# Unread products ahead of each tile of the MLPs' first products, and second products in three matmuls per block

## The chip, the cores and the metric

The kernel runs on one core of one Trainium2 chip. The metric is the device time of one execution in microseconds (us). The core has a tensor engine (PE in the profile, its weight loads as PEld), a vector engine (DVE), a scalar engine (ACT), a general engine (POOL) and an engine that issues transfers (SP).

## The reference

One launch computes three transformer layers on 256 tokens of width 1024: `first_block` (one layer) and `second_block` (two layers and a last norm). Each layer is a mixer with a residual and an MLP with a residual, and the MLP is what the change touches:

```python
D_FF = 4 * D_MODEL
...
        h = _rmsnorm(x, ln_mlp_g[l])
        x = x + jnp.square(jax.nn.relu(h @ w_mlp_up[l])) @ w_mlp_down[l]
...
def squared_relu_mlp(h, w_up, w_down):
    return jnp.square(jax.nn.relu(h @ w_up)) @ w_down
...
        x = x + squared_relu_mlp(rmsnorm(x, norm_mlp[layer]), w_up[layer], w_down[layer])
```

So there are three MLPs. In each the first product takes 1024 features to 4096, the second takes 4096 back to 1024. Everything is fp32.

## The kernel before, in words

**Layout.** Activations lie feature by feature: `x` is eight blocks of 128 features (partitions) by 256 tokens (columns). All weights stand in one stream `w` of 128x128 blocks in the order in which they are used. `load` (L134, on SP) brings two units of eight blocks into a tile `stg`; `take` splits a unit into two parts whose sum is the fp32 value: ACT writes the high part `whi` (L185), DVE the rest `wlo` (L187), both of type fp32r, which TensorE takes at one pass. Activations are split in the same way (`xh` and `xl`, one tile named `xo`; `hid` in the MLPs).

**One product of blocks.** `gemm` makes one output tile of 128 features by 256 tokens in a bank of PSUM (`pg`). For each block of weights it issues three matmuls of 256 columns: high weights by high activations (L242), high by low (L245), low by high (L246). Each matmul instruction loads its 128x128 weights anew (its LDWEIGHTS is in the profile as PEld). `gemm1` makes one such tile, `gemm2` two in one tile of PSUM, `gemm_tokens` (L281) makes tiles with the two operands in each other's place: activations are loaded, weights are streamed.

**The MLP** (`mlp`, three times: `mlp("norm_mix0")`, `mlp("norm_mix1")`, `mlp(None)`; MLP 1, 2 and 3 below). The first products are 16 calls of `gemm2`, so 32 output tiles of 8 blocks each, 256 blocks. ACT and DVE then make `hid` from each pair. The second products are 8 output tiles of 32 blocks each, again 256 blocks, followed by the residual. So each half of an MLP is 256 blocks, and with three matmuls per block it is 768 matmuls.

**The wide form.** In the second products `WIDE_NOT` says for how many of the eight tiles `gemm` is used. For MLP 1 and MLP 3 it is all eight; for MLP 2 it is one, and the other seven tiles go through `gemm_wide`: two matmuls per block, one of 512 columns (high weights by both parts of `hid`, L254) and one of 256 columns (L255). Its result stands in two halves, which an ACT copy (L400) and a DVE addition (L401) bring together.

**What sets the order.** The tile framework schedules the instructions of each engine from the program; PE runs them in that order. Other matmuls of the kernel, which the prediction uses for comparison, are fp32 products, which the profile shows as two records each: the sums of squares (L339 and L340, 128x256, weights of ones), `rstd_tokens` (L352, one column), and `decays` (L756, 128 columns). L961 is a lone fp32r product of 256 columns in the second mixer.

Of the kernel before, what the change touches and what calls it, by code (L numbers as in the profile page):

```python
# [10 lines left out]
FP32 = mybir.dt.float32  # L11
# [3 lines left out]
AF = mybir.ActivationFunctionType  # L15
ALU = mybir.AluOpType
PSUM = bass.MemoryType.PSUM

T = 256
D = 1024  # L20
FF = 4096
KD = 8
# [11 lines left out]
UNIT = 8  # L34
CHUNK_UNITS = 2

WIDE_NOT = {"norm_mix0": 8, "norm_mix1": 1, None: 8}

FIRST = 256

# [3 lines left out]
LEAD = 16  # L44
ROOM = 128
MIXED = 56

GROUPS_MIX = [range(0, 8)]
GROUPS_ATT = [range(0, 4), range(4, 6), range(6, 8)]
# [31 lines left out]
def kernel(  # L81
# [11 lines left out]
    nc = tc.nc  # L93
    nosync = mybir.DependencyInfo(mybir.DependencyClass.NoSync, mybir.DependencyReason.DATA)

    def after(first, last):
        if last is not None:
            tc.add_manual_dep(first.ins, last.ins.name, nosync)

    def pool(name, bufs=1, space=None, stack=ctx):  # L100
        kw = {"space": space} if space is not None else {}
        return stack.enter_context(tc.tile_pool(name=name, bufs=bufs, **kw))
# [7 lines left out]
    pg_p = pool("pg", 4, PSUM)  # L110
# [10 lines left out]
    def placed(t, n, at):  # L121

        return t[:, at:at + n * T].rearrange("p (k t) -> p k t", k=n)

    xh, xl = placed(xo, KD, LEAD), placed(xo, KD, LEAD + KD * T)
    cst = keep.tile([128, NCONST], FP32, name="cst")
    ones = keep.tile([128, 128], FP32, name="ones")
# [10 lines left out]
    a = 0  # L138
    for k, cols in ((2, slice(0, FIRST)), (5, slice(FIRST, UW)), (8, slice(UW, CW))):
# [3 lines left out]
        a = e  # L143
# [24 lines left out]
    units = {}  # L168
# [6 lines left out]
    def take(u, pieces=2):  # L175

        c, i = divmod(u, CHUNK_UNITS)
        if c not in staged:
            load(c)
        src = staged[c][:, i * UW:(i + 1) * UW]  # L180
        h = whi_p.tile([128, UW], FP32R, name="whi")
        l = wlo_p.tile([128, UW], FP32R, name="wlo")
        n = UW // pieces
        pieces = [slice(q * n, (q + 1) * n) for q in range(pieces)]
        act = [nc.scalar.activation(out=h[:, z], in_=src[:, z], func=AF.Copy)  # L185
               for z in (pieces if u == 0 else [slice(0, UW)])]
        dve = [nc.vector.tensor_tensor(out=l[:, z], in0=src[:, z], in1=h[:, z], op=ALU.subtract) for z in pieces]  # L187
        chain = hold.pop(0) if hold else None
        if chain:
            after(act[0], chain[0])  # L190
            after(dve[0], chain[1])
        units.clear()
        units[u] = h, l

    def block(n=1):

        b = stream["block"]
        stream["block"] = b + n
        u, i = divmod(b, UNIT)
        assert i + n <= UNIT  # L200
        if u not in units:
            take(u)
        h, l = units[u]
        return h[:, i * 128:(i + n) * 128], l[:, i * 128:(i + n) * 128]
# [13 lines left out]
    def step():  # L218
        for c in list(chains):
            if next(c, "end") == "end":  # L220
                chains.remove(c)

    def slot(steps=1):
        for d in list(due):
            d[0] -= 1
            if d[0] <= 0:
                due.remove(d)
                d[1]()
        credit[0] = credit[0] + steps if chains else 0
        while credit[0] >= 1:  # L230
            credit[0] -= 1
            step()

    def drain():
        while due or chains:
            slot()

    def gemm(ps, ks, ah, al, prev=None):

        for k in ks:  # L240
            h, l = block()
            m0 = nc.tensor.matmul(out=ps, lhsT=h, rhs=ah[:, k], start=(k == ks[0]), stop=False)  # L242
            if k == ks[0]:
                after(m0, prev)
            nc.tensor.matmul(out=ps, lhsT=h, rhs=al[:, k], start=False, stop=False)  # L245
            m1 = nc.tensor.matmul(out=ps, lhsT=l, rhs=ah[:, k], start=False, stop=(k == ks[-1]))  # L246
        return m1

    def gemm_wide(kt, a):

        ps = pg_p.tile([128, 2, T], FP32, name="pg")
        for k in range(kt):
            h, l = block()
            nc.tensor.matmul(out=ps, lhsT=h, rhs=a[:, k], start=(k == 0), stop=False)  # L254
            nc.tensor.matmul(out=ps[:, 1], lhsT=l, rhs=a[:, k, 0], start=False, stop=(k == kt - 1))  # L255
        slot(kt / KD)
        return ps

    def gemm1(kt, ah, al, steps=1):
        ks = kt if isinstance(kt, range) else range(kt)  # L260
        ps = pg_p.tile([128, 2, T], FP32, name="pg")
        gemm(ps[:, 0], ks, ah, al)
        slot(steps * len(ks) / KD)
        return ps[:, 0]

    def gemm2(kt, ah, al):
        ps = pg_p.tile([128, 2, T], FP32, name="pg")
        m = gemm(ps[:, 0], range(kt), ah, al)
        gemm(ps[:, 1], range(kt), ah, al, prev=m)
        slot(2 * kt / KD)  # L270
        return ps
# [72 lines left out]
    rvar = keep.tile([128, T], FP32, name="rvar")  # L344
# [25 lines left out]
    def mlp(gain_next):  # L370
        def variance():
            u = tmp.tile([128, 512], FP32, name="rs_u", bufs=1)[:, 0:T]
            nc.vector.tensor_scalar(out=u, in0=sum_squares(), scalar1=1.0 / D, scalar2=EPS, op0=ALU.mult, op1=ALU.add)
            nc.vector.reciprocal(out=rvar, in_=u)

        variance()
        with ExitStack() as st:
            hp = pool("hid", stack=st)
            mp = pool("mlpt", 2, stack=st)
            hid = hp.tile([128, FF // 128, 2, T], FP32R, name="hid")  # L380
            for j in range(0, FF // 128, 2):
                ps = gemm2(KD, xh, xl)
                r = mp.tile([128, 2, T], FP32, name="r")
                s = mp.tile([128, 2, T], FP32, name="s")
                nc.scalar.activation(out=r, in_=ps, func=AF.Relu)
                nc.scalar.activation(out=hid[:, j:j + 2, 0], in_=r, func=AF.Square)
                nc.vector.scalar_tensor_tensor(out=s, in0=ps, scalar=0.0, in1=r, op0=ALU.max, op1=ALU.mult)
                nc.vector.tensor_tensor(out=hid[:, j:j + 2, 1], in0=s, in1=hid[:, j:j + 2, 0], op=ALU.subtract)
            for j in range(KD):

                wide = j < KD - WIDE_NOT[gain_next]
                if wide:
                    ps = gemm_wide(FF // 128, hid)
                else:
                    ps = gemm1(FF // 128, hid[:, :, 0], hid[:, :, 1])

                for z in HALVES if gain_next is None and j == KD - 1 else [slice(0, T)]:
                    t = tmp.tile([128, T], FP32, name="dn")[:, z]
                    if wide:
                        nc.scalar.activation(out=t, in_=ps[:, 1], func=AF.Copy)  # L400
                        nc.vector.tensor_tensor(out=t, in0=ps[:, 0], in1=t, op=ALU.add)  # L401
                    nc.vector.tensor_tensor(out=t, in0=t if wide else ps[:, z], in1=rvar[:, z], op=ALU.mult)  # L402
                    nc.vector.tensor_tensor(out=x[:, j, z], in0=t, in1=x[:, j, z], op=ALU.add)  # L403
                    if z.stop - z.start < T:
                        nc.scalar.activation(out=rstd[:, z], in_=x[:, j, z], func=AF.Square)  # L405
                if gain_next is not None:
                    operand(j, gain_next)
                    squares(j)
                else:
                    if j < KD - 1:  # L410
                        squares(j)
                    nc.scalar.activation(out=xg[:, j], in_=x[:, j], func=AF.Copy, scale=v_("norm_final", j))  # L412
# [132 lines left out]
    with ExitStack() as st:  # L545
# [14 lines left out]
        ps = gemm1(KD, xh, xl)  # L560
# [159 lines left out]
        for j in range(0, 4, 2):  # L720
            ps = gemm2(KD, xh, xl)
            z = hg.tile([128, 2, T], FP32, name="hz", bufs=1)
# [83 lines left out]
        for j in range(4):  # L806
# [4 lines left out]
            t = hg.tile([128, T], FP32, name="ut", bufs=2)  # L811
# [8 lines left out]
            t = hg.tile([128, T], FP32, name="ut", bufs=2)  # L820
# [9 lines left out]
        for b, (yh, yl) in enumerate(((yc_h, yc_l), (ya_h, ya_l), (yh_h, yh_l))):  # L830
            if b == 2:
                while "linear" not in events:
                    slot()
                mhp = pool("mixh", stack=late)
                mh = placed(mhp.tile([128, KD * T + ROOM], FP32R, name="mh"), KD, MIXED)
                ml = placed(mhp.tile([128, KD * T + ROOM], FP32R, name="ml"), KD, MIXED)
            gates = {}
# [9 lines left out]
            for j in range(0, KD, 2):  # L847
                if j + 2 < KD:
                    gate(j + 2)
                ps = gemm2(4, yh, yl)  # L850
# [22 lines left out]
    for turn in (4096.0, 1.0):  # L873
# [4 lines left out]
        for i in range(6):  # L878
            m, e = math.frexp(rest)
# [14 lines left out]
    with ExitStack() as st:  # L894
# [10 lines left out]
        ps = gemm1(KD, xh, xl)  # L905
# [82 lines left out]
    with ExitStack() as st:  # L988
# [95 lines left out]
        ps = gemm1(KD, xh, xl)  # L1084
        scaled(kr[0:32], ps[0:32])
        a, b = rope(kr, 32)
# [4 lines left out]
        for j in range(2):  # L1091
            ps = gemm1(3, cqh, cql, RA)
            zr = att.tile([128, T], FP32, name="zr", bufs=2)
            nc.scalar.activation(out=zr, in_=ps, func=AF.Copy, scale=mscale)
            a, b = rope(zr, 128)
            for i in range(4):
                nc.vector.tensor_tensor(out=qm[64:96, 4 * j + i], in0=a[32 * i:32 * i + 32], in1=b[32 * i:32 * i + 32],
                                        op=ALU.add)
        for j in range(4):
            ps = gemm1(3, cqh, cql, RA)  # L1100
# [5 lines left out]
        for j in range(4):  # L1106
            ps = gemm1(2, ckh, ckl, rate[0])
# [22 lines left out]
    for z, (pool_, name) in zip(HALVES, ((po_p, "po"), (sc_p, "sc"))):  # L1130
        ps = pool_.tile([128, 512], FP32, name=name)[:, 0:T // 2]
# [204 lines left out]
```

## Time and profile before

| what | us |
|---|---|
| median of 3 runs | 1070.21 |
| lowest and highest of the runs | 1070.03 and 1076.8 |
| the profiled execution | 1071.9 |
| span of the profiled execution (first to last instruction) | 1070.1 |
| PE busy in the span | 1046.7 (98%) |
| DVE, ACT, POOL busy | 830.4, 597.9, 161.3 |
| mean granted TensorE clock, share of full speed | 0.995 |

The profile is of one execution. Busy times of PE add up matmuls that overlap, so the rate of PE is read from the distance between the starts of its instructions and not from its busy share. MLP 1 stands at about 289 to 467 us of the span, MLP 2 at 597 to 767, MLP 3 at 894 to 1060; the second half of each begins at about 376, 676 and 980 us.

### The profile page before, as it was taken

The numbers are of one execution on the slowest core, as the hardware profiler recorded it, in microseconds if no ns is written. First come the engines' busy times: TensorE is split into PE (matmuls) and PEld (weight loads), VectorE is DVE, ScalarE is ACT, GpSimd is POOL, SyncE is SP. The second block draws the span as 40 slices with busy tenths as digits, with TensorE's granted clock in tenths as the row PEclk, the third lists the DMA queues.
The fourth block names the chain that finished last, engine by engine and source line by source line (L and its number), as shares of the span: only waits on it lengthen the run. The fifth ranks groups of instructions, "written<-read, shape, count | busy, mean of one in ns | idle before, by whom it ended". The sixth has DMA issues, their size and how long they took to land. (4 is left out here: it accounts for less than half of the span.)

```text
span 1070.1 us, 21172 instructions
## 1 busy us (share of the span) xinstructions
PE 1046.7 (98%) x8584; PEld 1025.5 (96%) x8584; DVE 830.4 (78%) x1599; ACT 597.9 (56%) x930; POOL 161.3 (15%) x174
## 2 busy tenths in 40 slices
PE   7999999999999999999999999999999999999996
PEld 6999998999999999999999999988999999999996
DVE  7999898987897666669878977666699789776563
ACT  6467456666475544446655565444458755555441
POOL 1044651110500001120001200011121013000120
PEclk9999999999999999999999999999999999999998
DMA  8644433455445555555343555555454334555541
GB/s 291 225 159 153 148 130 119 163 197 181 174 173 200 181 195 177 190 189 193 119 157 122 196 197 190 175 190 194 158 182 156 136 112 156 205 193 183 197 179 40
DMA packets 29010, 183.99 MB, mean 172 GB/s; under 512 B 3056, under 2 KB 6384, under 8 KB 7280
## 3 DMA queue, kind: packets, MB, share of 16 engines
q1 hardware_dynamic: 28768, 182.50, 48.1%
q8 instruction: 67, 1.10, 0.4%
q14 instruction: 31, 0.25, 0.1%
q10 hardware_dynamic: 144, 0.13, 0.0%
HBM read 181.57 MB, written 1.05 MB: 171 GB/s over the span
## 5 line engine op out<-in xcount | busy, mean ns | idle before, releaser
L187 DVE TENSOR_TENSOR wlo<-stg,whi 128x512 fp32r<-128x512 f32 (+1 forms) x676 | 469.7, 736 | 156.9 <-ACT whi L185 152.3
L185 ACT ACTIVATE whi<-stg 128x1024 fp32r<-128x1024 f32 (+1 forms) x340 | 356.1, 1051 | 327.4 <-PE pg L245 266.1
L242 PE MATMUL pg<-xo,whi 128*128 128x256 f32 x1472 | 415.0, 283 | 8.3 <-ACT whi L185 7.3
L245 PE MATMUL pg<-xo,whi 128*128 128x256 f32 x1472 | 413.9, 282 | 0.6 <-DVE xo L319 0.6
L246 PE MATMUL pg<-xo,wlo 128*128 128x256 f32 x1472 | 413.9, 282 | 0.4 <-DVE wlo L187 0.2
L242 PEld LDWEIGHTS pg<-xo,whi 128*128 128x128 f32 x1472 | 278.9, 190 | 9.6 <-ACT whi L185 7.6
L245 PEld LDWEIGHTS pg<-xo,whi 128*128 128x128 f32 x1472 | 279.6, 190 | 2.2 <-DVE xo L319 1.3
L246 PEld LDWEIGHTS pg<-xo,wlo 128*128 128x128 f32 x1472 | 278.5, 189 | 1.9 <-DVE wlo L187 1.5
L246 PE MATMUL pg<-hid,wlo 128*128 128x256 f32 x544 | 151.6, 279 | 0.0
L245 PE MATMUL pg<-hid,whi 128*128 128x256 f32 x544 | 151.6, 279 | 0.0
L242 PE MATMUL pg<-hid,whi 128*128 128x256 f32 x544 | 151.6, 279 | 0.0
L245 PEld LDWEIGHTS pg<-hid,whi 128*128 128x128 f32 x544 | 103.2, 190 | 0.0
L242 PEld LDWEIGHTS pg<-hid,whi 128*128 128x128 f32 x544 | 102.3, 188 | 0.0
L246 PEld LDWEIGHTS pg<-hid,wlo 128*128 128x128 f32 x544 | 102.1, 188 | 0.0
L254 PE MATMUL pg<-hid,whi 128*128 128x512 f32 x224 | 79.2, 397 | 0.0
L327 POOL TENSOR_TENSOR sqa<-xv 128x256 f32<-128x256 f32 x6 | 5.0, 831 | 455.5 <-DVE xv L403 291.2
L255 PE MATMUL pg<-hid,wlo 128*128 128x256 f32 x224 | 62.9, 281 | 0.0
L331 POOL TENSOR_TENSOR sq<-xv 128x256 f32<-128x256 f32 x36 | 29.9, 836 | 173.5 <-DVE xv L403 160.5
L254 PEld LDWEIGHTS pg<-hid,whi 128*128 128x128 f32 x224 | 42.1, 188 | 10.4
L281 PE MATMUL pg<-whi,xo 128*128 128x256 f32 x256 | 47.4, 282 | 0.0
L255 PEld LDWEIGHTS pg<-hid,wlo 128*128 128x128 f32 x224 | 42.0, 188 | 0.0
L281 PEld LDWEIGHTS pg<-whi,xo 128*128 128x128 f32 x256 | 39.5, 188 | 0.1
(356 smaller groups left out, 1599.1 us busy)
## 6 DMA issues: line engine op xcount, KB each, us to landing
stg<-w SPq DMA_DIRECT2D x168, 1024.0 KB, 4.8
t<-t_bias SPq DMA_DIRECT2D x8, 128.0 KB, 3.0
cb<-chk_bias SPq DMA_DIRECT2D x1, 1024.0 KB, 4.8
xv<-x_in SPq DMA_DIRECT2D x2, 384.0 KB, 6.7
cst<-consts SPq DMA_DIRECT2D x1, 640.0 KB, 11.2
stg<-w SPq DMA_DIRECT2D x1, 512.0 KB, 8.1
out<-xg SPq DMA_DIRECT2D x2, 256.0 KB, 2.5
stg<-w SPq DMA_DIRECT2D x1, 384.0 KB, 6.8
```

The lines of the kernel that those rows point to most:

```text
L185: act = [nc.scalar.activation(out=h[:, z], in_=src[:, z], func=AF.Copy) for z in (pieces if u == 0 else [slice(0, UW)])]
L187: dve = [nc.vector.tensor_tensor(out=l[:, z], in0=src[:, z], in1=h[:, z], op=ALU.subtract) for z in pieces]
L242: m0 = nc.tensor.matmul(out=ps, lhsT=h, rhs=ah[:, k], start=(k == ks[0]), stop=False)
L245: nc.tensor.matmul(out=ps, lhsT=h, rhs=al[:, k], start=False, stop=False)
L246: m1 = nc.tensor.matmul(out=ps, lhsT=l, rhs=ah[:, k], start=False, stop=(k == ks[-1]))
L254: nc.tensor.matmul(out=ps, lhsT=h, rhs=a[:, k], start=(k == 0), stop=False)
L255: nc.tensor.matmul(out=ps[:, 1], lhsT=l, rhs=a[:, k, 0], start=False, stop=(k == kt - 1))
L281: nc.tensor.matmul(out=ps, lhsT=a[:, k, t], rhs=w_, start=(k == 0 and i == 0), stop=(k == kt - 1 and i == 2))
L327: nc.gpsimd.tensor_tensor(out=sqa, in0=x[:, j], in1=x[:, j], op=ALU.mult)
L331: nc.gpsimd.tensor_tensor(out=s, in0=x[:, j], in1=x[:, j], op=ALU.mult)
```

## The change

Two edits. First, `gemm` may issue an unread product ahead of the first matmul of a tile: `mlp` fills a list `between` with 32 entries, one for each tile of its first products, and empties it before the second products. The product writes the first columns of the tile's own bank, and the tile's first matmul then overwrites them. An entry is a kind, a number of columns n and, in some, how many times. The kind "dense" loads high weights and streams n columns of `xh`, "tokens" loads 128 columns of `xh` and streams n columns of the high weights (both fp32r), "exact" loads ones and streams n columns of constants (both fp32). Second, the wide form is gone: all second products are made of three matmuls per block.

```diff
-WIDE_NOT = {"norm_mix0": 8, "norm_mix1": 1, None: 8}
+B = ("tokens", 240)
+_ds = [("dense", 16), ("exact", 1), ("dense", 128), ("exact", 128), ("tokens", 128), ("dense", 100), ("tokens", 256), ("exact", 64)]
+BETWEEN = {
+    "norm_mix0": [k for d in _ds for k in (d, B, d, B)],
+    "norm_mix1": [k for d in _ds for k in (d, d, B, d)],
+    None: [k for d in (("tokens", 240, 2), ("tokens", 200), ("tokens", 136), ("tokens", 248), ("tokens", 256, 2),
+                       ("tokens", 256, 4), ("tokens", 224), ("tokens", 240, 3)) for k in (d, d, B, d)],
+}
...
+    between = []
+
+    def small(ps, prev):
+
+        kind, n, times = (between.pop(0) + (1,))[:3]
+        h = next(iter(units.values()))[0]
+        for _ in range(times):
+            a, b = {"tokens": (xh[:, 0, 0:128], h[:, 0:n]), "dense": (h[:, 0:128], xh[:, 0, 0:n]),
+                    "exact": (ones, cst[:, 0:n])}[kind]
+            m = nc.tensor.matmul(out=ps[:, 0:n], lhsT=a, rhs=b, start=True, stop=True)
+            after(m, prev)
+            prev = m
+        return prev
+
     def gemm(ps, ks, ah, al, prev=None):
 
         for k in ks:
             h, l = block()
+            if k == ks[0] and between:
+                prev = small(ps, prev) if between[0] else between.pop(0) or prev
             m0 = nc.tensor.matmul(out=ps, lhsT=h, rhs=ah[:, k], start=(k == ks[0]), stop=False)
...
+            between[:] = BETWEEN[gain_next]
             for j in range(0, FF // 128, 2):
                 ps = gemm2(KD, xh, xl)
...
+            between.clear()
             for j in range(KD):
-
-                wide = j < KD - WIDE_NOT[gain_next]
-                if wide:
-                    ps = gemm_wide(FF // 128, hid)
-                else:
-                    ps = gemm1(FF // 128, hid[:, :, 0], hid[:, :, 1])
+                ps = gemm1(FF // 128, hid[:, :, 0], hid[:, :, 1])
```

`gemm_wide` itself, the ACT copy and the DVE addition that belonged to it are removed.

The lines of `gemm` move: L242, L245 and L246 of before are L266, L269 and L270 of after, and an unread product has L255. PE of after, at a border of two tiles in the first products of MLP 1, where the product is an "exact" one of one column (`cst` and `ones` are its operands, the number behind `pg` tells the two tiles of PSUM apart):

```order
L270 MATMUL pg_3741<-xo_87,wlo_3775 128x256
L255 MATMUL pg_3810<-cst_88,ones_89 128x1
L266 MATMUL pg_3810<-xo_87,whi_3811 128x256
L269 MATMUL pg_3810<-xo_87,whi_3811 128x256
L270 MATMUL pg_3810<-xo_87,wlo_3812 128x256
```

One product stands between the last matmul of one tile and the first of the next, and it writes the next tile's bank; before, the two tiles followed each other there without it. Each of the 96 tiles of the three first halves gets such an entry. 84 entries are one product, the other 12 (all in MLP 3) two, three or four in a row, which makes 32 products in MLP 1, 32 in MLP 2 and 53 in MLP 3. 15 of them are "exact" (6 in MLP 1, 9 in MLP 2), 102 are fp32r.

PE of before, at the border from the first to the second products of MLP 2 (`hid` is the hidden activations, the 128x512 rows are the wide form):

```order
L245 MATMUL pg<-xo,whi 128x256
L246 MATMUL pg<-xo,wlo 128x256
L254 MATMUL pg<-hid,whi 128x512
L255 MATMUL pg<-hid,wlo 128x256
L254 MATMUL pg<-hid,whi 128x512
```

PE of after, inside the same second products:

```order
L270 MATMUL pg<-hid,wlo 128x256
L266 MATMUL pg<-hid,whi 128x256
L269 MATMUL pg<-hid,whi 128x256
L270 MATMUL pg<-hid,wlo 128x256
L266 MATMUL pg<-hid,whi 128x256
```

The 224 blocks that had two matmuls have three, and the number of columns per block is the same 768.

## Rows read from the trace of the kernel before

**Rows 1.** Windows, MLP stretches: busy us (instructions) by engine, clock, DMA share, GB/s.

```profile
300.00:374.00 74.00, 74.00 (x630) 74.00 (x630) 56.00 (x95) 45.56 (x57) 0.00 (x0) 1.00 0.55 198
677.00:754.00 77.00, 77.00 (x438) 66.86 (x437) 50.71 (x81) 34.23 (x42) 9.01 (x11) 1.00 0.53 189
985.00:1058.00 73.00, 73.00 (x647) 73.00 (x646) 40.06 (x61) 28.11 (x31) 12.39 (x13) 1.00 0.42 147
```

**Rows 2.** First matmul of each block in seven MLP stretches: count, ns, first and last start.

```profile
L242 PE MATMUL pg<-xo,whi x210: 281/281/281, 299.8 to 373.7; 128*128 128x256 f32 x105
...
L242 PE MATMUL pg<-hid,whi x241: 281/281/281, 380.0 to 464.8; 128*128 128x256 f32 x121
...
L242 PE MATMUL pg<-xo,whi x213: 276/276/276, 601.7 to 673.9; 128*128 128x256 f32 x107
...
L254 PE MATMUL pg<-hid,whi x219: 397/397/398, 676.6 to 753.7; 128*128 128x512 f32 x110
...
L242 PE MATMUL pg<-hid,whi x29: 281/281/281, 755.8 to 765.7; 128*128 128x256 f32 x29
...
L242 PE MATMUL pg<-xo,whi x216: 276/276/276, 899.7 to 972.8; 128*128 128x256 f32 x108
...
L242 PE MATMUL pg<-hid,whi x216: 276/276/276, 984.7 to 1057.8; 128*128 128x256 f32 x108
```

**Rows 3.** Timeline of PE around L352, four one-column records: start, us, what.

```profile
477.36 0.50 PE L352 MATMUL sc<-cst,rstd 128*128 128x1 f32 x4
477.72 0.48 PE L281 MATMUL pg<-whi,xo 128*128 128x256 f32 x2
478.04 0.28 PE L281 MATMUL pg<-wlo,xo 128*128 128x256 f32 x1
```

**Rows 4.** Timeline of PE around L756, eight records of 128 columns.

```profile
126.12 1.05 PE L756 MATMUL sc<-mm 128*128 128x128 f32 x8
126.93 0.37 PE L246 MATMUL pg<-xo,wlo 128*128 128x256 f32 x1
127.13 0.28 PE L242 MATMUL pg<-xo,whi 128*128 128x256 f32 x1
```

**Rows 5.** Timeline of PE around L340, one fp32 product of 256 columns.

```profile
289.52 0.39 PE L242 MATMUL pg<-xo,whi 128*128 128x256 f32 x2
...
289.86 0.28 PE L246 MATMUL pg<-xo,wlo 128*128 128x256 f32 x1
289.98 0.59 PE L340 MATMUL po<-sq,ones 128*128 128x256 f32 x2
290.22 0.47 PE L242 MATMUL pg<-xo,whi 128*128 128x256 f32 x1
290.52 0.28 PE L245 MATMUL pg<-xo,whi 128*128 128x256 f32 x1
...
290.88 0.28 PE L245 MATMUL pg<-xo,whi 128*128 128x256 f32 x1
```

**Rows 6.** Timeline of PE around L961, one fp32r product of 256 columns.

```profile
491.07 0.28 PE L242 MATMUL pg<-xo,whi 128*128 128x256 f32 x1
...
491.41 0.28 PE L242 MATMUL pg<-xo,whi 128*128 128x256 f32 x1
...
491.87 0.28 PE L961 MATMUL sc<-fparts,row 128*128 128x256 f32 x1
...
492.35 0.28 PE L245 MATMUL pg<-xo,whi 128*128 128x256 f32 x1
...
492.69 0.28 PE L245 MATMUL pg<-xo,whi 128*128 128x256 f32 x1
```

**Rows 7.** Timeline of PE from L281 (operands in each other's place) back to L242.

```profile
779.01 0.40 PE L281 MATMUL pg<-whi,xo 128*128 128x256 f32 x2
...
779.37 0.28 PE L242 MATMUL pg<-xo,whi 128*128 128x256 f32 x1
...
779.72 0.28 PE L242 MATMUL pg<-xo,whi 128*128 128x256 f32 x1
...
780.06 0.28 PE L242 MATMUL pg<-xo,whi 128*128 128x256 f32 x1
```

More of the change, by code (lines that the diff above doesn't have):

```diff
@@ L247, in gemm @@
         return m1
[L249 to L257, printed above, removed]
     def gemm1(kt, ah, al, steps=1):
@@ L388, in mlp @@
                 nc.vector.tensor_tensor(out=hid[:, j:j + 2, 1], in0=s, in1=hid[:, j:j + 2, 0], op=ALU.subtract)
+            between.clear()
             for j in range(KD):
-                wide = j < KD - WIDE_NOT[gain_next]
-                if wide:
-                    ps = gemm_wide(FF // 128, hid)
-                else:
-                    ps = gemm1(FF // 128, hid[:, :, 0], hid[:, :, 1])
+                ps = gemm1(FF // 128, hid[:, :, 0], hid[:, :, 1])
                 for z in HALVES if gain_next is None and j == KD - 1 else [slice(0, T)]:
                     t = tmp.tile([128, T], FP32, name="dn")[:, z]
[L399 to L402, printed above, removed]
+                    nc.vector.tensor_tensor(out=t, in0=ps[:, z], in1=rvar[:, z], op=ALU.mult)
                     nc.vector.tensor_tensor(out=x[:, j, z], in0=t, in1=x[:, j, z], op=ALU.add)
```

## The prediction

> **What bounds the kernel now.** I read the windows first. In the MLPs PE is busy in all of every stretch at the full clock, 2.4 GHz (granted share 1.00), while DVE works 40 to 56 and ACT 28 to 46 of the 73 to 77 us of a stretch [rows 1]. So nothing that ACT or DVE lose or win in an MLP counts, and every nanosecond by which PE's instructions stand further apart is on the path that sets the end.
>
> The second view is the first matmul of each block, with count and first and last start. The distance of two blocks is the last start minus the first, over the count less one [rows 2]. The first half of MLP 1 gives 73.9 / 209 = 0.3536 us, its second half 84.8 / 240 = 0.3533; the first half of MLP 2 72.2 / 212 = 0.3406; the wide form 77.1 / 218 = 0.3537; the one unwide tile behind it 9.9 / 28 = 0.3536; MLP 3 73.1 / 215 = 0.3400 in both halves. Same instructions, same operands' shapes, same clock, and two cadences: 0.340 us a block (113.3 ns a matmul) and 0.3535 (117.8 ns), each kept over hundreds of matmuls. I call them fast and slow. A half of an MLP is 256 blocks, so slow costs it 256 x 0.0134 = 3.4 us. Of the six halves three are slow (both of MLP 1, the second of MLP 2).
>
> Third, the timeline at odd instructions, to see what ends a cadence. One fp32 product (L340) turns fast into slow: three steps take 289.86 - 289.52 = 0.34 us before it and 290.88 - 290.52 = 0.36 after it [rows 5]; MLP 1 starts there and stays slow. A lone fp32r product of 256 columns leaves fast as it is: 491.41 - 491.07 = 0.34 before L961, 492.69 - 492.35 = 0.34 after [rows 6]. The step from L281 back to L242, operands in each other's place, turns slow into fast: 779.37 - 779.01 = 0.36, then 780.06 - 779.72 = 0.34 [rows 7]. So the change acts twice: it takes PE's time, and at 96 places it draws the cadence anew.
>
> **The products' own time.** An fp32 product of few columns is two records. Four one-column records and two ordinary matmuls take 478.04 - 477.36 = 0.68 us; less two slow matmuls of 0.118 that leaves 0.444, or 0.111 a record [rows 3]. Eight records of 128 columns and one ordinary matmul take 127.13 - 126.12 = 1.01 us, 0.112 each [rows 4]. So one column costs what 128 cost: below 256 columns each record has its own weights to load, and takes 0.112 us. There are 102 fp32r products (26 in MLP 1, 23 in MLP 2, 53 in MLP 3) with one record each, and 15 "exact" ones with two: 132 x 0.112 = **14.8 us**. No row shows an fp32r product under 256 columns. From below: if it cost only its columns, at the ordinary 0.113 / 256 us a column, the 21,452 columns of the fp32r products come to 9.5 us, and the 965 columns of the "exact" ones to 1.6, by L340, which with the next matmul takes 290.52 - 289.98 = 0.54 us, so 0.42 alone for 256 columns [rows 5]; together 11.1. From above: if it went at the fp32 rate of L340, a product of 240 columns would take 0.39 us, and all of them together with the 0.224 that a narrow fp32 product takes at least come to 33 us. I take 14.8, by the nearest rows in shape (128x128 weights, one record).
>
> [...]
>
> **Settling.** Behind an odd instruction the next few steps are some 10 ns long in sum: from L242 at 779.37 to 779.72 three take 0.35 where the fast cadence has 0.34 [rows 7]. 96 places x 0.010 = **1.0 us**.
>
> **The cadence after it.** This is the uncertain term; each half can win or lose 3.4 us. I carry over three rules from the rows: "exact" leaves slow, fp32r in a fast stretch leaves fast, "tokens" (L281's form) in a slow stretch brings fast. For narrow ones the last has no row; I let it work half the time.
> - MLP 1, first half (slow before): 6 tiles behind "exact" are slow, half of the "tokens" tiles that follow them stay slow, and some of the next; with the start some 12 of 32. 20 / 32 become fast: -2.1 us.
> - MLP 1, second half: no products, so it keeps what the last tile drew. That is B behind "exact", even odds: -1.7.
> - MLP 2, first half (fast before): 9 "exact" tiles, 1 or 2 of the B tiles, some 3 behind these; 13 of 32 become slow: +1.4.
> - MLP 2, second half: the last entry is "exact", so slow. Three slow matmuls take the 0.3536 of the unwide tile where the wide pair takes 0.3537 [rows 2]: 224 blocks, 0.0. Were it fast, -3.4. The ACT copy and DVE addition that go stand beside a busy PE: 0.
> - MLP 3, both halves (fast before): only "tokens", fast stays fast: 0.
> Sum -2.4. From both sides: all six halves fast, -10.2; all slow, +10.2.
>
> **Sum.** 14.8 + 1.0 - 2.4 = +13.4 us. On the profiled execution's 1071.9 (span 1070.1) that is 1085.3; this execution is 1.7 above the median of the runs, and on 1070.2 it is 1083.6. I say **1084 us**. The unread products fill no idle time: PE has none in the MLPs, and the weights they use are already there. What they give ACT and DVE, a few us more per MLP, nobody waits for.
>
> **The rivals.**
> - *Slow wins.* Narrow products mostly leave the slow cadence, in MLP 3 as well. For it: L340, and that nothing in the rows shows a narrow product bringing fast. Against it: L961 and L281. 14.8 + 1.0 + 4 to 10 = +20 to +26 on the median: 1090 to 1096.
> - *Not slower by what can be told: fast wins.* One mechanism, at the tile borders: the operands in each other's place (87 of the 117 products) bring fast as at 779.37, and "exact" does not undo it because it is followed by B or by a short record. Then all six halves are fast: 14.8 + 1.0 - 10.2 = +5.6, or 1075.8. It counts as within 1% from a cadence term of -5.1 on, that is 1.5 of the three slow halves freed net. For it: rows 6 and 7, in which fp32r products leave or bring fast. Against: L340, and MLP 2's last entry.
> - *Columns only.* A narrow fp32r product costs its columns, 11.1 in all: 11.1 + 1.0 - 2.4 = +9.7, or 1079.9. Against it: rows 3 and 4. [...]
> - *Fp32 rate.* A narrow fp32r product goes as fp32: 33 + 1.0 - 2.4 = +32, or 1102. For it: every fp32r matmul that the trace shows has 256 columns or more, so none speaks against it. Against: nothing in the two records' form says that the rate hangs on the columns.
> - *The change does nothing:* unread products that were moved off the path or dropped would leave the time alone. PE's order has them in place, so there is no room for this.
>
> **Chances.** A change of under 1%, 10.7 us, is about what a measurement of this kernel can't tell from none. Forecast (mixed, +9 to +18): 0.57, of which a sixth lies under +10.7. Slow wins: 0.21. Fast wins: 0.12. Columns only: 0.04. Fp32 rate: 0.06. Slower by over 1%: 0.47 + 0.21 + 0.06 = 0.74; within 1%: 0.10 + 0.12 + 0.04 = 0.26, of which I leave 0.01 for faster, which would need a cadence that no long stretch of the trace has. The range goes from all fast to all slow, 1076 to 1096, and leaves out the fp32 rate; the forecast's own is 1079 to 1088.
>
> **What would show it.** In the profile of the changed kernel: the records at L255 stand about 0.112 us before the next matmul, whatever their columns, and an "exact" one is two of them; blocks of L266 stand 0.340 or 0.3535 apart and change only at tile borders; tiles behind "exact" are slow, tiles behind a repeated "tokens" fast; the second halves keep the cadence of the last tile of the first; MLP 2's second half has 0.3535. It is wrong if the steps at L255 hang on the columns (0.4 us for 240, or a few ns for 16), if a third cadence appears, if a tile changes its cadence in the middle, or if PE waits at L255 for something.

## The result, and the profile after

The changed kernel takes **1084.34 us** (median of 7 runs, 1082.99 to 1084.98), before 1070.91 (7 runs, 1070.03 to 1076.98). The ratio is 1.0109, with an interval of 1.0085 to 1.0134. Some runs of before, and of several experiments, come out 5 to 7 us above the others of the same kernel; the medians stand well below these, and no profile shown here is of such a run. The profiled execution takes 1083.66 us with a span of 1081.9, against 1071.9 and 1070.1 before, so the two profiles stand 11.8 us apart.

The windows of the three MLP stretches, in the columns of [rows 1]:

```profile
300.00:374.00 74.00, 74.00 (x642) 74.00 (x641) 53.52 (x91) 44.16 (x56) 0.00 (x0) 1.00 0.54 190
685.00:769.00 84.00, 84.00 (x744) 84.00 (x743) 55.88 (x85) 37.20 (x40) 14.34 (x13) 1.00 0.56 198
987.00:1070.00 83.00, 83.00 (x735) 83.00 (x734) 46.27 (x71) 32.40 (x35) 12.39 (x13) 1.00 0.44 153
```

Nothing has changed in what bounds the MLPs: PE is busy in all of each stretch at a granted clock of 1.00, DVE and ACT are not. So the time sits in the distances of PE's instructions again. Here is the first matmul of each block of the second halves (MLP 1, 2, 3), as in [rows 2]:

```profile
L266 PE MATMUL pg<-hid,whi x244: 281/281/282, 380.0 to 465.9; 128*128 128x256 f32 x122
...
L266 PE MATMUL pg<-hid,whi x248: 276/276/277, 684.8 to 768.8; 128*128 128x256 f32 x124
...
L266 PE MATMUL pg<-hid,whi x245: 276/276/277, 987.0 to 1069.9; 128*128 128x256 f32 x123
```

85.9 / 243 = 0.3535 us, 84.0 / 247 = 0.3401 and 82.9 / 244 = 0.3398: slow, fast, fast. MLP 2's second half was slow in before and was forecast slow. The reader sees the cadence in the matmul's own duration as well: 281 ns where it is slow, 276 where it is fast.

For a ledger I take each half from start to start: a first half from its first matmul on `xo` to the first on `hid`, a second half from there to the start of the last on `hid`. For MLP 3 these are in before

```profile
883.61 0.28 PE L242 MATMUL pg<-xo,whi 128*128 128x256 f32 x1
...
973.16 0.28 PE L242 MATMUL pg<-hid,whi 128*128 128x256 f32 x1
...
1060.09 0.28 PE L246 MATMUL pg<-hid,wlo 128*128 128x256 f32 x1
```

and in after

```profile
887.88 0.28 PE L266 MATMUL pg<-xo,whi 128*128 128x256 f32 x1
...
984.92 0.28 PE L266 MATMUL pg<-hid,whi 128*128 128x256 f32 x1
...
1071.85 0.28 PE L270 MATMUL pg<-hid,wlo 128*128 128x256 f32 x1
```

so 89.55 and 86.93 us before, 97.04 and 86.93 after. A product ahead of the very first matmul of a half stands outside this count, so 31 of the 32 places of a first half are in it. The same for every kernel of this study (first / second half, us; one profiled execution each):

| kernel | MLP 1 | MLP 2 | MLP 3 |
|---|---|---|---|
| before | 92.36 / 90.33 | 89.71 / 90.33 | 89.56 / 86.93 |
| after | 95.30 / 90.34 | 95.76 / 86.93 | 97.03 / 86.93 |
| e1_no_products | 92.33 / 90.34 | 89.71 / 86.93 | 89.56 / 86.93 |
| e2_products_only | 95.30 / 90.33 | 95.74 / 90.33 | 97.11 / 86.93 |
| e3_one_flip | 89.39 / 86.93 | 89.79 / 86.93 | 89.56 / 86.93 |
| e4_two_flips | 92.39 / 90.34 | 89.71 / 86.93 | 89.56 / 86.93 |
| e5_narrow16 | 95.21 / 86.93 | 95.49 / 90.34 | 95.28 / 90.33 |
| e6_wide256 | 96.01 / 90.34 | 93.07 / 86.93 | 92.93 / 86.93 |
| e7_exact1 | 96.42 / 86.93 | 96.50 / 86.93 | 96.43 / 86.93 |
| e8_set248 | 90.64 / 86.93 | 89.83 / 86.93 | 89.89 / 86.93 |
| e9_set_exact64 | 90.05 / 86.93 | 89.95 / 86.93 | 89.92 / 86.93 |
| e10_shift1 | 98.88 / 86.93 | 99.00 / 90.34 | 98.86 / 90.34 |
| e11_shift2 | 103.22 / 90.33 | 103.25 / 90.34 | 101.96 / 90.34 |
| e12_exact256 | 92.79 / 90.34 | 93.13 / 90.33 | 92.95 / 90.34 |

A second half is 86.93 us or 90.33, with nothing between: fast or slow as a whole. After minus before: +2.94, 0, +6.05, -3.40, +7.47, 0, together +13.06. The first mixer, which the change doesn't touch, is 1.55 us shorter in after's profile; its length goes from 282.3 to 284.1 us over the profiles of the twelve kernels that leave it alone (all but e8 and e9), and before's was the longest. The rest, 0.3, lies between the MLPs.

Now the products. One of 128 columns at a border where the cadence turns from slow to fast, on PE of after (start us, us, engine, line):

```profile
330.95 0.28 PE L266 MATMUL pg<-xo,whi 128*128 128x256 f32 x1
...
331.31 0.23 PE L255 MATMUL pg<-whi,xo 128*128 128x128 f32 x1
331.37 0.33 PE L266 MATMUL pg<-xo,whi 128*128 128x256 f32 x1
331.54 0.28 PE L269 MATMUL pg<-xo,whi 128*128 128x256 f32 x1
331.66 0.28 PE L270 MATMUL pg<-xo,wlo 128*128 128x256 f32 x1
331.77 0.28 PE L266 MATMUL pg<-xo,whi 128*128 128x256 f32 x1
...
332.11 0.28 PE L266 MATMUL pg<-xo,whi 128*128 128x256 f32 x1
```

The product starts only 0.06 us before the next matmul, but that one then takes longer, and the two together take 331.54 - 331.31 = 0.23: 0.115 each. The block before it took 331.31 - 330.95 = 0.36 us, the second one behind it 332.11 - 331.77 = 0.34. And an "exact" product of one column, in a fast tile:

```profile
610.45 0.28 PE L266 MATMUL pg<-xo,whi 128*128 128x256 f32 x1
...
610.79 0.28 PE L255 MATMUL pg<-cst,ones 128*128 128x1 f32 x2
610.93 0.36 PE L266 MATMUL pg<-xo,whi 128*128 128x256 f32 x1
611.13 0.28 PE L269 MATMUL pg<-xo,whi 128*128 128x256 f32 x1
...
611.35 0.28 PE L266 MATMUL pg<-xo,whi 128*128 128x256 f32 x1
...
611.69 0.28 PE L266 MATMUL pg<-xo,whi 128*128 128x256 f32 x1
```

Two records and the next matmul take 611.13 - 610.79 = 0.34 us, and the blocks take 0.34 before and behind: fast stayed fast.

I went through the 96 borders of after in this way. What each product turned its tile's cadence into, where the tile was undisturbed by other work:

| product | from fast | from slow |
|---|---|---|
| "tokens" 240, once | slow, 23 of 23 | fast, 6 of 6 |
| "tokens" and "dense" of 100 to 224, "tokens" 256, once | slow, 7 of 7 | fast, 21 of 21 |
| "tokens" 248 | fast, 2 of 2 | fast, 1 of 1 |
| "exact" 64 and 128 | fast, 4 of 4 | fast, 6 of 6 |
| "exact" 1 | fast, 2 of 2 | slow, 2 of 2 |
| "tokens" 256, two or four in a row | slow, 3 of 3 | slow, 3 of 3 |
| "tokens" 240, three in a row | fast, 1 of 1 | slow, 2 of 2 |

So most single fp32r products **toggle** the cadence, a few forms **set** it fast, and tiles 1 to 32 draw their cadence from a chain of such steps. 15, 18 and 13 of the 32 tiles of the first halves are fast (the first few of each MLP, which other work interrupts, are counted by their larger part). There is one exception to the toggle, and it is not in after: in the trace of e2, whose products are the same, one "tokens" of 200 columns (908.41 us, MLP 3) stands between two slow tiles, where after has a slow and a fast one. So the list of products alone does not fix the chain.

### The profile page after: what moved, and what is told of

It is laid out like the page before. It is cut to its first block, busy times and chain, and to the rows that moved or that the text cites. A ratio compares the mean times of both kernels' runs of the same rounds, so it can differ in the third digit from the quotient of the medians.

```text
span 1081.9 us, 21869 instructions
## 1 busy us (share of the span) xinstructions
PE 1058.8 (98%) x8940; PEld 1047.4 (97%) x8940; DVE 830.8 (77%) x1592; ACT 597.3 (55%) x923; POOL 163.3 (15%) x174
## 5 line engine op out<-in xcount | busy, mean ns | idle before, releaser
L266 PE MATMUL pg<-xo,whi 128*128 128x256 f32 x1472 | 418.1, 285 | 7.5 <-ACT whi L193 7.2
L269 PE MATMUL pg<-xo,whi 128*128 128x256 f32 x1472 | 414.2, 282 | 0.3 <-DVE xo L333 0.2
L270 PE MATMUL pg<-xo,wlo 128*128 128x256 f32 x1472 | 413.0, 281 | 0.2
L266 PEld LDWEIGHTS pg<-xo,whi 128*128 128x128 f32 x1472 | 278.5, 189 | 8.7 <-ACT whi L193 7.5
L269 PEld LDWEIGHTS pg<-xo,whi 128*128 128x128 f32 x1472 | 278.7, 189 | 2.1 <-DVE xo L333 1.4
L270 PEld LDWEIGHTS pg<-xo,wlo 128*128 128x128 f32 x1472 | 277.3, 189 | 1.4 <-DVE wlo L195 0.9
L266 PE MATMUL pg<-hid,whi 128*128 128x256 f32 x768 | 213.3, 278 | 0.0
L269 PE MATMUL pg<-hid,whi 128*128 128x256 f32 x768 | 213.3, 278 | 0.0
L270 PE MATMUL pg<-hid,wlo 128*128 128x256 f32 x768 | 213.3, 278 | 0.0
L269 PEld LDWEIGHTS pg<-hid,whi 128*128 128x128 f32 x768 | 145.3, 189 | 0.0
L266 PEld LDWEIGHTS pg<-hid,whi 128*128 128x128 f32 x768 | 144.2, 188 | 0.0
L270 PEld LDWEIGHTS pg<-hid,wlo 128*128 128x128 f32 x768 | 144.2, 188 | 0.0
L345 POOL TENSOR_TENSOR sq<-xv 128x256 f32<-128x256 f32 x36 | 32.5, 909 | 168.3 <-DVE xv L411 154.8
L475 ACT ACTIVATE p<-p,m 128x128 f32<-128x128 f32 x64 | 28.6, 448 | 19.3 <-DVE m L473 19.2
L403 DVE TENSOR_TENSOR hid<-s,hid 128x512 fp32r<-128x512 f32 x48 | 33.2, 691 | 5.3 <-ACT hid L401 1.2
L346 POOL TENSOR_TENSOR sqa<-sqa,sq 128x256 f32<-128x256 f32 x36 | 36.6, 1016 | 2.4
L269 PE MATMUL pg<-ol,whi 128*128 128x256 f32 x128 | 36.4, 286 | 0.2 <-DVE ol L305 0.2
```

The source lines that it names most:

```text
L345: nc.gpsimd.tensor_tensor(out=s, in0=x[:, j], in1=x[:, j], op=ALU.mult)
L346: nc.gpsimd.tensor_tensor(out=sqa, in0=sqa, in1=s, op=ALU.add)
L475: nc.scalar.activation(out=p[:, a:b], in_=p[:, a:b], func=AF.Exp, scale=-1.0, bias=m[:, i:i + 1], accum_out=sums[:, i:i + 1])
```

## The experiments

All but e2 have after's second edit (three matmuls per block) and differ in the list of products alone. "flip" below is `("tokens", 240)`, once.

**e1: no products at all.**

```diff
+BETWEEN = {"norm_mix0": [], "norm_mix1": [], None: []}
```

> No unread products, all second products as three matmuls per block (the second edit alone). Theory 'history': a cadence, once drawn, stays until an odd instruction, so MLP 2's second half goes on in the fast cadence of its first half: 86.9 us instead of 90.3, and the whole 3.4 us under the kernel before, about 1067.5 against 1070.9. Rival 'operands': the second products of MLP 2 are slow whatever form they have, since the wide pair and the one unwide tile both took 0.3536 a block: no change, 1070.9.

Measured 1067.61 us (10 runs, 1066.37 to 1074.24), 0.9956 of before (0.9927 to 0.9985). MLP 2's second half:

```profile
L260 PE MATMUL pg<-hid,whi x245: 276/276/276, 677.9 to 760.8; 128*128 128x256 f32 x123
```

82.9 / 244 = 0.3398 us a block, where the wide pair took 0.3537 [rows 2], and every other half is as before. So the second edit alone gains 3.4 us, and it is the cadence that gains them: the 0.340 of the first half carries over. The wide form was what made that half slow, not the number of matmuls.

**e2: the products alone**, with before's wide form put back.

```diff
-                ps = gemm1(FF // 128, hid[:, :, 0], hid[:, :, 1])
+                if wide:
+                    ps = gemm_wide(FF // 128, hid)
+                else:
+                    ps = gemm1(FF // 128, hid[:, :, 0], hid[:, :, 1])
```

> The changed kernel with the wide form kept in seven tiles of MLP 2's second products (the first edit alone). The wide pair took 0.3537 a block before and should again, whatever cadence the products leave: 90.3 us instead of 86.9 in that half, 3.4 more than the changed kernel, about 1087.7. Rival 'operands' (already weakened by the kernel without products): no difference, 1084.3.

Measured 1087.47 us (2 runs), 1.0155 (1.0125 to 1.0184). The products alone cost 16.7 us, the second edit alone gains 3.3 to 3.6, and 16.7 - 3.4 = 13.3 is the change: the two edits add up. MLP 2's second half is wide, at 74.2 / 210 = 0.3533 us, though the first half handed over the same cadence as in after:

```profile
L279 PE MATMUL pg<-hid,whi x211: 397/398/398, 685.6 to 759.8; 128*128 128x512 f32 x106
```

**e3 and e4: one flip, and two.** Does a flip bring fast, or does it toggle? MLP 1 is slow when it comes.

```diff
+    "norm_mix0": [None, None, None, B],
```

> The same as the kernel without products, with one unread product of 240 columns (tokens) in all: ahead of the fourth tile of MLP 1. Theory 'history and flip': a single narrow fp32r product turns slow into fast, and nothing turns it back, so 28 tiles of MLP 1's first half and all of its second half run at 0.340 a block: 89.4 and 86.9 us, 6.3 us less than without it, about 1061.2. Rival 'place': MLP 1 is slow because of its operands or of what ACT, DVE and the transfers do beside it, and the product moves its own tile alone: about 1067.6.

Measured 1061.70 us (7 runs, 1060.46 to 1067.71), 0.9902 (0.9865 to 0.9938). One product of 0.11 us frees 6 us: both halves of MLP 1 become fast, 89.39 and 86.93 for 92.33 and 90.34.

```diff
+    "norm_mix0": [None, None, None, B, None, B],
```

> As with one product, and a second one of the same kind two tiles later (fourth and sixth tile of MLP 1). Theory 'flip': the second turns fast back into slow, two tiles are fast, the rest of MLP 1 slow: first half about 92.4, second 90.3, in all about 1067.6. Rival 'tokens brings fast' (the rule that the prediction used): the second changes nothing, MLP 1 stays fast: about 1061.3.

Measured 1067.48 us (8 runs, 1066.80 to 1074.48), 0.9963 (0.9930 to 0.9996), what e1 takes without any. The first flip on PE,

```profile
293.16 0.28 PE L260 MATMUL pg<-xo,whi 128*128 128x256 f32 x1
293.51 0.28 PE L249 MATMUL pg<-whi,xo 128*128 128x240 f32 x1
293.63 0.28 PE L260 MATMUL pg<-xo,whi 128*128 128x256 f32 x1
293.98 0.28 PE L260 MATMUL pg<-xo,whi 128*128 128x256 f32 x1
294.32 0.28 PE L260 MATMUL pg<-xo,whi 128*128 128x256 f32 x1
```

and the second, two tiles on:

```profile
298.40 0.28 PE L260 MATMUL pg<-xo,whi 128*128 128x256 f32 x1
298.74 0.28 PE L260 MATMUL pg<-xo,whi 128*128 128x256 f32 x1
299.08 0.27 PE L249 MATMUL pg<-whi,xo 128*128 128x240 f32 x1
299.19 0.28 PE L260 MATMUL pg<-xo,whi 128*128 128x256 f32 x1
299.55 0.28 PE L260 MATMUL pg<-xo,whi 128*128 128x256 f32 x1
299.90 0.28 PE L260 MATMUL pg<-xo,whi 128*128 128x256 f32 x1
```

Blocks of 0.35 become 0.34 behind the first product and 0.35 to 0.36 behind the second. The same product, placed twice, undoes itself. "Tokens brings fast", which I had carried over from [rows 7], falls.

**e5, e6, e7: one kind on all 96 tiles**, for the price of a narrow, an ordinary and a two-record product.

```diff
+BETWEEN = {m: [("dense", 16)] * 32 for m in ("norm_mix0", "norm_mix1", None)}
```

> One dense product of 16 columns ahead of every tile of the first products of all three MLPs, 96 in all. Theory 'weights': each takes the 0.112 us of its weights, 10.8 us in all and about 1 us of settling; theory 'flip': every other tile is slow, 32 flips are an even number, so each second half keeps the cadence in which the MLP began: against the kernel without products +10.8 + 1.0 - 1.7 + 1.7 + 1.7 = +13.5, about 1081. Rival 'columns only': 16 columns are 0.007 us each, 0.7 in all, so with the same flips +2.4 to +3.4, about 1070.5.

Measured 1085.99 us (2 runs), 1.0114 (1.0045 to 1.0183): the rival by columns is out, and my own number missed by 5 us. The flip does not alternate. Here are the products ahead of two fast tiles (304.66 and 316.33), each followed by the next product; two products between 307.51 and 316.33 are left out:

```profile
304.66 0.17 PE L249 MATMUL pg<-xo,whi 128*128 128x16 f32 x1
...
307.51 0.17 PE L249 MATMUL pg<-xo,whi 128*128 128x16 f32 x1
...
316.33 0.17 PE L249 MATMUL pg<-xo,whi 128*128 128x16 f32 x1
...
319.18 0.17 PE L249 MATMUL pg<-xo,whi 128*128 128x16 f32 x1
```

A fast tile takes 2.85 us, the three tiles after it 316.33 - 307.51 = 8.82, or 2.94 each, and the next 2.85: one fast, three slow, and again. From fast all 23 undisturbed products led to slow; from slow 22 led to fast and 40 stayed slow. Averaged over the slow tiles at one place of that cycle of four, the steps from matmul to matmul are not alike: of any three in a row one takes 118.3 ns and the others 117.5 (by the starts in the trace, which are kept to 1 ns; the rows here show 10 ns). A tile of 24 matmuls and one product moves the next product by one step, so slow would let go at one of its three steps alone. That was the new theory ("three steps"); a rival was that tiles take turns in PSUM buffers. The price is seen in a fast tile: 2.85 - 8 x 0.340 = 0.13 us with the settling, for 16 columns.

```diff
+BETWEEN = {m: [("dense", 256)] * 32 for m in ("norm_mix0", "norm_mix1", None)}
```

> One unread dense product of 256 columns ahead of every tile of the first products, 96 in all: in form it is an ordinary first matmul, with the same weights and the first block of activations. Theory 'form': it is one more matmul of the cadence it stands in and flips nothing: 32 x 0.1178 + 64 x 0.1133 = 11.0 us over the kernel without products, about 1078.6, first halves 96.1, 93.3 and 93.2, second halves 90.3, 86.9 and 86.9. Rival 'anything extra flips': cadences change at the tile borders as with 16 columns, and the second halves differ from 90.3, 86.9, 86.9.

Measured 1078.02 us (8 runs, 1077.66 to 1084.19), 1.0061 (1.0034 to 1.0089). A product in the stream's own form turns nothing, and costs (93.07 - 89.71) / 31 = 0.108 us in fast and (96.01 - 92.33) / 31 = 0.119 in slow, about one step of the cadence. MLP 1 stays slow to its end:

```profile
L260 PE MATMUL pg<-hid,whi x245: 281/281/282, 381.8 to 468.0; 128*128 128x256 f32 x123
```

```diff
+BETWEEN = {m: [("exact", 1)] * 32 for m in ("norm_mix0", "norm_mix1", None)}
```

> One unread exact product (fp32) of one column ahead of every tile, 96 in all. Theory 'left as it was' (from the changed kernel, where the one-column fp32 product left slow slow and fast fast): MLP 1 stays slow, MLP 2 and 3 fast; two records of 0.112 each: 96 x 0.224 = 21.5 us over the kernel without products, about 1089; second halves 90.3, 86.9, 86.9. Rival 'exact leaves slow' (the prediction's rule): both halves of MLP 2 and 3 slow as well, 13.6 more, about 1103.

Measured 1082.39 us (8 runs, 1081.11 to 1082.91), 1.0077 (1.0051 to 1.0104). Fast stayed fast at all of the 82 undisturbed products, and the price is (96.43 - 89.56) / 31 = 0.222 us, two records of 0.111. What I missed is that MLP 1 became fast, which makes most of the 7 us between forecast and run. The one undisturbed product that met slow led to fast (294.0 us); the four in after and e2 that met slow at another step left it slow.

**e8 and e9: a setter.** By the table, "tokens" 248 and "exact" 64 lead to fast from either cadence. One stands ahead of the fourth tile of each MLP, and one ahead of a product of the first mixer.

```diff
+SET = ("tokens", 248)
+BETWEEN = {m: [None, None, None, SET] for m in ("norm_mix0", "norm_mix1", None)}
...
+            if b == 2 and j == 0:
+                between[:] = [SET]
             ps = gemm2(4, yh, yl)
```

> Four unread products in all, tokens of 248 columns: ahead of the fourth tile of each MLP, and ahead of the first of the last up-products in the first mixer (about 200 us). In the changed kernel 248 columns left fast fast (twice) and turned slow fast (once). Theory 'setter': each of these stretches runs fast whatever it was before: against the kernel with one flip (1061.7) another 3.2 us less from the first mixer's end, about 1058.5, and its runs that lie 6 us higher are gone. Rival 'one case was luck': from other steps of the slow cadence it stays slow, and MLP 1 or the mixer's end is at 0.3535 a block: 1061 to 1068, with runs 6 us higher.

Measured 1060.37 us (4 runs, 1059.58 to 1061.32), 0.9873 (0.9832 to 0.9913). e9 has `("exact", 64)` in its place:

> The same four places with one exact product of 64 columns each, which in the changed kernel turned slow fast (three times) and left fast fast (twice). Theory 'setter': about 1058.9 (each costs two records), no runs 6 us higher. Rival 'fp32 leaves slow' (the prediction's rule, from L340): MLP 1 slow, and MLP 2 and 3 turned slow as well: about 1082.

Measured 1060.36 us (4 runs, 1059.79 to 1061.08), 0.9875 (0.9827 to 0.9923). In both, all six halves are fast; MLP 1's second half in e8:

```profile
L261 PE MATMUL pg<-hid,whi x245: 276/276/276, 374.0 to 457.0; 128*128 128x256 f32 x123
```

83.0 / 244 = 0.3402 us for 0.3533 [rows 2]. These two are the fastest kernels of the study, 10.9 us below before. That they set fast from any point of the slow cadence is not shown: over all traces 15 such products met slow, and all led to fast, but all met it with the 118.3 ns step second or third to last before them. The 200-column product of e2 that left slow alone had it last. The mixer's product gave less than I expected (1058.5), since part of it is given back at once: MLP 1's first half takes 90.64 us for e3's 89.39. In e8's timeline the start of MLP 1 has a wait that before's does not show there:

```profile
283.76 0.39 PE L264 MATMUL pg<-xo,whi 128*128 128x256 f32 x1 [0.79 <-DVE xo L328]
```

PE, early now, waits 0.79 us for DVE's `xo`.

**e10, e11: which step the product meets.** One or two ordinary "dense" 256 ahead of the "dense" 16 of e5. They turn nothing (e6), but make 26 and 27 matmuls a tile for 25.

```diff
-        for _ in range(times):
+        last = n
+        for i in range(times):
+            n = last if i == times - 1 else T
...
+BETWEEN = {m: [("dense", 16, 2)] * 32 for m in ("norm_mix0", "norm_mix1", None)}
```

> One ordinary unread product of 256 columns and then one of 16 ahead of every tile. In the kernel with 16 columns alone the tiles went fast, slow, slow, slow and so on: a flip out of slow at every third product that met slow, each time at the same step of slow's cycle of three. Theory 'three steps': with 26 matmuls from product to product instead of 25 the steps met are 1, 0, 2 in place of 0, 1, 2, and 2 is the one that flips: again one fast tile in four. About 11 us over 1086, some 1097. Rival 'buffers' (the period of four comes from four buffers of PSUM or the weights' buffers): one in four as well; this run only tells with the next.

Measured 1096.48 us (one run): every fourth tile fast, as expected. Here again are the products ahead of two fast tiles, each followed by the next (L251, x2 for the two of a place):

```profile
306.45 0.29 PE L251 MATMUL pg<-xo,whi 128*128 128x256 f32 x2
...
309.42 0.28 PE L251 MATMUL pg<-xo,whi 128*128 128x256 f32 x2
...
318.58 0.29 PE L251 MATMUL pg<-xo,whi 128*128 128x256 f32 x2
...
321.56 0.28 PE L251 MATMUL pg<-xo,whi 128*128 128x256 f32 x2
```

2.97 us fast, 9.16 for the three slow tiles, 2.98 fast. e11 has `("dense", 16, 3)`:

> Two ordinary unread products of 256 columns and then one of 16 ahead of every tile. Theory 'three steps': with 27 matmuls from product to product the first product in slow meets step 2 and flips, so every other tile is fast; about 22 us over 1086 less 2.6, some 1105. Rival 'buffers': one fast tile in four, as before, since the tiles' buffers are the same; about 1108.

Measured 1110.88 us (one run). 27 is nine whole blocks, so the product meets the same step in every tile. In MLP 3, which is entered fast, tiles alternate (products L251, x3 for the three of a place, of which the first two have 256 columns):

```profile
955.56 0.40 PE L251 MATMUL pg<-xo,whi 128*128 128x256 f32 x3
...
958.73 0.41 PE L251 MATMUL pg<-xo,whi 128*128 128x256 f32 x3
...
961.82 0.40 PE L251 MATMUL pg<-xo,whi 128*128 128x256 f32 x3
...
964.98 0.41 PE L251 MATMUL pg<-xo,whi 128*128 128x256 f32 x3
...
968.07 0.40 PE L251 MATMUL pg<-xo,whi 128*128 128x256 f32 x3
```

3.17, 3.09, 3.16, 3.09 us: slow, fast, slow, fast. PSUM buffers taken in turn have no reason to make a period of four with 25 and 26 matmuls and of two with 27; steps of three have. The 118.3 ns step shows it directly: over e5, e10 and e11 the 16-column product let go of slow in all 57 undisturbed cases where that step was the second to last before it, and in none of the 136 others. My time was too low by 6 us mostly because MLP 1 and MLP 2 went slow, within their interrupted first tiles, at a step that does not let go (the long one third to last in MLP 1, last in MLP 2), and then met that step in every tile: no later tile is fast, 103.22 and 103.25 us.

**e12: the fp32 product of 256 columns.** [Rows 5] had shown one that turned fast to slow, while "exact" 64 and 128 set fast.

```diff
+SET = ("exact", 256)
+BETWEEN = {m: [None, None, None, SET] for m in ("norm_mix0", "norm_mix1", None)}
```

> One exact product (fp32) of 256 columns ahead of the fourth tile of each MLP, three in all. Before, the fp32 product of 256 columns (L340) turned fast into slow, and the prediction carried that over to 'exact' of fewer columns, which left fast fast in every case since. Theory 'the columns decide': at 256 it leaves slow in all three MLPs, four fast halves lost against the kernel without products, about 1067.6 + 13 = 1080. Rival 'fp32 leaves fast fast at any width': MLP 2 and 3 stay fast: 1068 to 1069, or 1062 where MLP 1 turns fast.

Measured 1080.85 us (2 runs), 1.0093 (1.0064 to 1.0122). Three products cost 13 us against e1: MLP 2 and MLP 3 turn from fast to slow, MLP 1 stays slow. The second halves of MLP 2 and 3:

```profile
L261 PE MATMUL pg<-hid,whi x250: 281/281/282, 680.0 to 767.9; 128*128 128x256 f32 x125
...
L261 PE MATMUL pg<-hid,whi x247: 281/281/282, 980.9 to 1067.8; 128*128 128x256 f32 x124
```

## Why the prediction was right, and where it was not

The time, 1084.0 forecast and 1084.34 measured, and the sum of the halves, +13.4 forecast and +13.06 in the profiles, came out. Not all of the steps did: the products' price was understood, the cadence was not, and that its terms came to nearly the forecast sum was luck.

- *What bounds the kernel* held: no engine but PE counts, and the time lies in two cadences at one clock. e3 shows it best, with 6 us from one product. But MLP 1 does not turn slow at L340. In before's trace it begins at 284.1 us, not 289, and its matmuls stand 118 ns apart from the first; the fast stretch ahead of L340 is six matmuls long. That one fp32 product of 256 columns turns a long fast stretch slow was shown only by e12.
- *The products' own time* (14.8, and 1.0 of settling) was near. In after, a tile costs 8 x 0.0134 = 0.107 us more when slow; 15, 18 and 13 fast tiles for about 0, 32 and 32 of before make -1.6, +1.5 and +2.0 us. What is left of +2.94, +6.05 and +7.47 is 4.5, 4.6 and 5.5, together 14.5 for the 128 records inside the halves (four stand ahead of them): 0.113 each with the settling, where the forecast's figures give 15.3 for these. That 16 columns cost what 256 do, 0.11 to 0.13 us, is shown by e5 and e6; "columns only" and "fp32 rate" are out. Wrong was the sign given for it, that the records "stand about 0.112 us before the next matmul, whatever their columns": a product of 128 stands 0.06 before it, and the next matmul makes up the rest.
- *The cadence* came to -1.5 us for -2.4 forecast, but by other terms: first halves -1.6, +1.5 and +2.0 (forecast -2.1, +1.4, 0), second halves 0, -3.4 and 0 (forecast -1.7, 0, 0). Errors of +2.0, -3.4 and +1.7, with smaller ones, added up to only +0.9. The failed step is the one that says "I carry over three rules". "fp32r in a fast stretch leaves fast": it does at 256 columns in the stream's form (e6) and at 248, but a narrower one led to slow 23 times of 23, and MLP 3 lost 2.0 us by it. "'exact' leaves slow": at 256 columns an fp32 product makes slow (e12), at 64 it makes fast (e9), at one it leaves fast alone (e7). "'tokens' in a slow stretch brings fast": half of a toggle (e4). The sign "tiles behind a repeated 'tokens' fast" failed too: of the nine such undisturbed tiles eight are slow.
- *MLP 2, second half*, "the last entry is 'exact', so slow": that entry is "exact" 64, a setter to fast. The 3.4 us set down there as "Were it fast, -3.4" came.
- *MLP 1, second half*: slow where I had even odds. As forecast, the second halves keep the cadence that the last tile drew; only which one it was failed.
- *The rivals*: "slow wins" has the loss in MLP 3 right and its size wrong, since a toggle gives back at the next border. "Fast wins" needed setters on most tiles; only 248 and "exact" 64 and 128 are such. "Fp32 rate" was added up wrong: at 0.42 us for 256 columns and no less than 0.224 for a narrow one, the fp32r products come to 36.6 us and the "exact" ones to 3.4, so 40 rather than 33, and the rival stood at about 1109.
- PE waited at L255 once, 0.5 us for DVE in all of the MLPs. This doesn't count beside 14.5.

One thing could have been seen beforehand. The rule for "exact" rested on L340 alone, and before's trace had a row against it. L756, of [rows 4], is fp32 and 128 columns wide, four products in a row, and leaves fast fast: a block took 0.34 us before it and 0.34 again behind it,

```profile
125.55 0.28 PE L242 MATMUL pg<-xo,whi 128*128 128x256 f32 x1
...
125.89 0.28 PE L242 MATMUL pg<-xo,whi 128*128 128x256 f32 x1
...
127.82 0.28 PE L242 MATMUL pg<-xo,whi 128*128 128x256 f32 x1
...
128.16 0.28 PE L242 MATMUL pg<-xo,whi 128*128 128x256 f32 x1
```

What stays open: why a form toggles or sets. The steps of a slow block explain when "dense" 16 lets go of slow, not why 248 columns differ from 240. That "exact" 1 also depends on the step rests on five products, of which one let go. Whether the setters work at the third step is open, and so is why several products in a row don't act as so many toggles. And where the first mixer's own 1.8 us of difference from execution to execution come from was not tried.

## What to carry to other kernels

Where PE is the bound, measure the distance of like matmuls before anything else: here the same stream ran at 113.3 or 117.8 ns a matmul for hundreds of microseconds, and one odd instruction decided which. Look then for the last odd instruction ahead of each long stretch, and try one cheap setter behind it; test it alone and twice, since a product that helps once may undo itself, and at more than one place, since the step of the cadence that it meets can matter. A rule about such a state that rests on one row is worth little; look in the trace for rows against it first, and remember that a sum of several wrong terms may come out right by chance.

## What was not expected of the hardware

- A product's column count and type decide what it does to the cadence, and little what it costs: 240 fp32r columns toggle, 248 set fast; 64 fp32 columns set fast, 256 turn fast to slow (from slow, 240, 248 and 64 were met at two of the three steps only); the fp32r ones that were measured alone (16 and 256 columns on all tiles) cost 0.11 to 0.13 us.
- The slow cadence has a cycle of three matmuls (118.3, 117.5, 117.5 ns) and "dense" 16 leaves it at one of the three only, 57 times of 57 there and never in 136 other cases: period four with 25 and 26 matmuls a tile, two with 27.
- The wide pair of 512 and 256 columns takes 0.3533 to 0.3537 us a block, both times behind a fast first half (before, e2): as much as three ordinary matmuls at the slow cadence, and 0.0135 us more than at the fast.
